# A two-layer hybrid decoder trunk: S5 preparation split into three steps, with its input projections and two gates spread over the attention heads

## The chip, the cores and the metric

The kernel runs on one core of one Trainium2 chip. The metric is the device time of one execution in microseconds (us). Shown for the kernel before are three timed runs and one profiled execution with its trace. The engines are TensorE (PE for its matmuls, PEld for its weight loads), VectorE (DVE), ScalarE (ACT), GpSimd (POOL) and SyncE (SP), which issues every DMA of this kernel.

## The reference, cut to what matters

Each of two layers normalises its input, makes one wide input projection of it, runs three token mixers side by side, gates and adds their outputs, projects the sum and adds it to the input. 512 tokens, width 1024, all in float32.

```python
for l in range(DEPTH):
    h = rms_norm(x, pre_norm[l])
    proj = h @ w_in[l]
    z_a, xbc, dt_raw, u_b, z_b, c_q, c_kv, k_rope, z_c, gate_logits = split_columns(proj)
    y_a = ssd_branch(z_a, xbc, dt_raw, ...) @ w_a[l]
    y_b = s5_branch(u_b, z_b, ...) @ w_b[l]
    y_c = mla_branch(c_q, c_kv, k_rope, z_c, ...) @ w_c[l]
    gates = jax.nn.sigmoid(gate_logits).reshape(bsz, s, N_BRANCH, D_MODEL)
    merged = gates[..., 0, :] * y_a + gates[..., 1, :] * y_b + gates[..., 2, :] * y_c
    x = x + rms_norm(merged @ w_o[l], post_norm[l])
```

The change touches two branches. MLA is latent attention with 16 heads: q and k/v come from normalised latents of rank 512 and 256, and each head runs a causal softmax over 512 positions. S5 is a complex diagonal state-space model over 64 groups of 16 channels with 64 states each. Its input is `u_b`, 1024 columns of the projection. The kernel computes it in chunks of 8 tokens: from powers of the diagonal it builds, for every group, a local response (kpad), an output operator (odr) and the state that each chunk adds (msd); a scan over 64 chunks follows later.

## The kernel before, in words

Every float32 operand is split into a high and a low part (`split`, line 83: an ACT copy and a DVE subtraction) and each product is three matmuls. `weight` (line 92) loads a 128x1024 weight tile into one of two `wf` buffers by a DMA on SP, and ACT and DVE (or, for every third tile in the MLA stage, POOL) split it; `dense` (line 108) then runs 24 matmuls of 512 columns into one of three main PSUM banks. `proj` (line 134) is `dense` on a tile of the input projection.

A layer (`layer`, line 980) runs two MLA latent projections and the small tail projection, then the MLA stage, then `mix` (line 1001): the softmax sums are divided out, the gates and output projections of MLA are merged, then SSD, S5 and the final projections. The S5 preparation, `s5_prep` (line 241), is a Python generator whose steps are placed among the attention work: `fill(n)` in `mla` (line 481) advances it n steps. It is called once before the latents (line 510), once between the two normalisations (line 513), and at the end of each head two times on even heads and three times on odd ones (line 601).

The first step computes the powers of the diagonal on DVE. Then each of eight blocks of eight groups takes five steps. `block(b)` (line 317) projects the S5 input tile, copies it to `pu`, writes it to DRAM (`ud`, line 322), reads it back in another order in eight DMAs of 16 partitions into `puf` (line 325), writes that to DRAM for later (`u2`, line 329), loads the B and C parameters `bc1`, `bc2` (lines 332 to 334), and forms `pbb`, `pbs` on POOL. `front(b, s)` (line 350), four times, builds on POOL the operators of two groups: `pw1`, `pv1`. `back(b, s)` (line 368), one step later, transposes `pw1` on PE into the bank `pm` (line 377), splits it into `pmh`, `pml`, multiplies these with the split input `pu2` into `pM` (lines 386, 387), and on every second step copies `pM` to `pmo`, makes the local responses `pk` (line 395, the same bank as `pm`), copies them to `pkf` and writes them to `kpad` (line 404). After four steps `pmo` goes to DRAM (line 406). `pu`, `puf` and `pmo` share two buffers (tag `pf`); `pmh` and `pml` have one each.

`gate` (line 446) projects one tile of gate logits and puts its tanh on ACT into one of seven shared `tmp` buffers; `gates_ahead` (line 452) makes gates that do not yet exist. `mix` begins with two MLA gates (line 1009).

The order written in Python is not the order on the engines. The kernel is built with `schedule_with_timeline_sim=True`: a planner orders the instructions of each engine by a simulated timeline, with the order written as priority, and each engine then works through its list in that fixed order. SP's DMA issues are such a list too.

## Time and profile before

| | us |
|---|---|
| median of 3 runs | 1980.36 (1975.66 to 1982.38) |
| the profiled execution | 1977.92 |
| its span, first to last instruction | 1976.1 |
| PE busy | 1870.3 (95%) |
| DVE busy | 1420.3 (72%) |
| ACT busy | 914.2 (46%) |
| POOL busy | 631.9 (32%) |
| mean granted TensorE clock | 0.967 |

The profiled execution is 2.4 us under the median, and 1.8 us of it lie outside the span. Busy time is counted per engine; matmuls overlap their weight loads, so PE and PEld stand side by side. A row of the windows view gives, for a stretch of the span, its length, the busy time of each engine with the number of instructions, the granted clock of PE as a share of full speed, the busy share of the DMA engines and the GB/s they moved. A row of the timeline gives start, length, engine, line, operation, tiles, shapes, count and, in brackets, the idle time before it and what ended it. A row of the waits view gives the total wait in us, how many waits, and the longest.

### The profile page before, as it was taken

To read this page: it belongs to the slowest core of one execution; us is meant where nothing else is said; L and a number is where in the kernel's file an instruction comes from. 1 tells how busy PE (TensorE), PEld (TensorE's weight loads), DVE (VectorE), ACT (ScalarE), POOL (GpSimd) and SP (SyncE) were. 2 spreads that over 40 slices of the span, in tenths; PEclk is the share of its full clock that TensorE was granted. 3 is DMA by queue.
4 is the path that set the end of the run, shared out by engine and by line. 5 is a ranking of instruction groups with operands and counts; after the bars stand their busy time and mean duration, and the time that the engine had idled before them with its cause. 6 is when DMAs were issued, how large, how long until landed. Compare 5 with 4: busy or idle time off the path is not lost.

```text
span 1976.1 us, 28153 instructions
## 1 busy us (share of the span) xinstructions
PE 1870.3 (95%) x9880; PEld 1528.1 (77%) x9880; DVE 1420.3 (72%) x2882; ACT 914.2 (46%) x1647; POOL 631.9 (32%) x679
## 2 busy tenths in 40 slices
PE   7898999899999989999998989999999999999998
PEld 5687777687877868888876877776878887788887
DVE  6866566799999857744578566667999996776443
ACT  4355455522555545533332555554235663554331
POOL 1746656201233201201118465661013331012010
PEclk9898998899999999999997999998999999999999
DMA  5343333322321266345233334343332224662541
GB/s 158 94 114 94 108 114 103 119 92 84 128 65 64 75 187 182 92 152 167 90 83 90 111 93 122 100 128 96 96 130 75 74 76 113 183 174 86 171 128 43
DMA packets 136253, 219.99 MB, mean 111 GB/s; under 512 B 39856, under 2 KB 79408, under 8 KB 135600
## 3 DMA queue, kind: packets, MB, share of 16 engines
q1 hardware_dynamic: 136112, 218.19, 37.1%
q8 instruction: 78, 1.28, 0.3%
q14 instruction: 63, 0.52, 0.1%
HBM read 182.08 MB, written 31.33 MB: 108 GB/s over the span
## 4 chain that ended last, share of the span: by engine, by line
PE 60%; DVE 22%; DMA 9%; ACT 3%; issue 2%; POOL 2%; SPq 2%; DVEq 0%; ACTq 0%; POOLq 0%
PE mm L116 15%; PE mm L117 14%; PE mm L119 14%; DMA wf<-in_w_in 3%; DVE wl L78 3%; DVE keep L69 3%; PE mm L61 2%; PE mm L62 2%; PE mm L63 2%; PE aux L61 1%; DVE tmp L69 1%; DVE ms L899 1%; PE aux L62 1%; PE aux L63 1%; DVE sc_t L896 1%
## 5 line engine op out<-in xcount | busy, mean ns | idle before, releaser
L116 PE MATMUL mm<-hh,wh 128*128 128x512 f32 (+1 forms) x1232 | 499.5, 405 | 11.5 <-ACT wh L66 8.0
L66 ACT ACTIVATE wh<-wf 128x1024 fp32r<-128x1024 f32 (+1 forms) x294 | 291.3, 994 | 440.2 <-PE mm L117 227.2
L117 PE MATMUL mm<-hl,wh 128*128 128x512 f32 (+1 forms) x1232 | 492.0, 399 | 0.0
L78 DVE TENSOR_TENSOR wl<-wf,wh 128x1024 fp32r<-128x1024 f32 (+1 forms) x243 | 294.8, 1218 | 188.1 <-ACT wh L66 154.3
L119 PE MATMUL mm<-hh,wl 128*128 128x512 f32 (+1 forms) x1232 | 314.9, 393 | 1.9 <-DVE wl L78 1.9
L116 PEld LDWEIGHTS mm<-hh,wh 128*128 128x128 f32 (+1 forms) x1232 | 236.5, 192 | 72.2 <-ACT wh L66 11.6
L117 PEld LDWEIGHTS mm<-hl,wh 128*128 128x128 f32 (+1 forms) x1232 | 236.2, 192 | 48.5 <-issue 0.5
L119 PEld LDWEIGHTS mm<-hh,wl 128*128 128x128 f32 (+1 forms) x1232 | 228.2, 188 | 52.6 <-DVE wl L78 2.3
L81 POOL TENSOR_TENSOR mg<-mg,tmp 128x512 f32<-128x512 f32 x32 | 77.7, 2431 | 458.1 <-DVE tmp L78 240.5
L81 POOL TENSOR_TENSOR wl<-wf,wh 128x1024 fp32r<-128x1024 f32 (+1 forms) x51 | 108.9, 2135 | 302.6 <-PE mm L119 209.3
L116 PE MATMUL mm<-ah,wh 128*128 128x512 f32 x512 | 200.3, 393 | 0.0
L117 PE MATMUL mm<-al,wh 128*128 128x512 f32 x512 | 199.9, 391 | 0.0
L119 PE MATMUL mm<-ah,wl 128*128 128x512 f32 x512 | 127.6, 390 | 0.0
L116 PEld LDWEIGHTS mm<-ah,wh 128*128 128x128 f32 x512 | 96.2, 188 | 21.4 <-ACT pkf L66 0.7
L117 PEld LDWEIGHTS mm<-al,wh 128*128 128x128 f32 x512 | 96.1, 188 | 20.9 <-issue 1.0
L119 PEld LDWEIGHTS mm<-ah,wl 128*128 128x128 f32 x512 | 95.7, 188 | 19.6
L617 DVE CUSTOM_DVE_ANT_0 sc<-aux,cmask 128x128 f32<-128x128 f32 (+3 forms) x128 | 60.9, 485 | 63.5 <-PE aux L63 62.5
L66 ACT ACTIVATE sc<-sc,nm 128x128 f32<-128x128 f32 (+3 forms) x128 | 70.4, 554 | 13.3 <-DVE nm L73 13.2
L81 POOL TENSOR_TENSOR pv<-pq,ar 128x288 f32<-128x288 f32 x64 | 49.1, 789 | 77.2 <-PE pk L395 68.7
L69 DVE SCALAR_TENSOR_TENSOR keep<-mm,cw,keep 128x511 f32<-128x511 f32 (+2 forms) x96 | 71.1, 740 | 2.0 <-ACT keep L66 1.5
L66 ACT ACTIVATE tmp<-mm 128x512 f32<-128x512 f32 x76 | 44.8, 592 | 56.2 <-PE mm L63 31.5
L81 POOL TENSOR_TENSOR pw<-pbb,ar 128x256 f32<-128x256 f32 x64 | 51.0, 799 | 41.8 <-PE pm L377 41.6
(346 smaller groups left out, 4002.8 us busy)
## 6 DMA issues: line engine op xcount, KB each, us to landing
wf<-in_w_in SPq DMA_DIRECT2D x156, 512.0 KB, 3.6
odr<-pv SPq DMA_DIRECT2D x64, 128.0 KB, 2.0
wf<-in_w_c SPq DMA_DIRECT2D x16, 512.0 KB, 3.4
wf<-in_w_a SPq DMA_DIRECT2D x16, 512.0 KB
wf<-kpad SPq DMA_DIRECT2D x128, 64.0 KB, 6.4
wf<-odr SPq DMA_DIRECT2D x16, 512.0 KB, 7.1
wf<-in_w_glu SPq DMA_DIRECT2D x16, 512.0 KB, 3.4
wf<-in_w_b SPq DMA_DIRECT2D x16, 512.0 KB, 3.8
```

Of the source, the lines that this page charges most:

```text
L61: mm(out, ah, bh, start=start, stop=False)
L62: mm(out, ah, bl, start=False, stop=False)
L63: mm(out, al, bh, start=False, stop=stop)
L66: self.nc.scalar.activation(out, in_, func, **kw)
L69: self.nc.vector.scalar_tensor_tensor(out, in0, s, in1, op0, op1)
L78: self.nc.vector.tensor_tensor(out, a, b, op)
L81: self.nc.gpsimd.tensor_tensor(out, a, b, op)
L116: mm(ps[:m], wh[:, o(i)], bh, start=i == 0, stop=False)
L117: mm(ps[:m], wh[:, o(i)], bl, start=False, stop=False)
L119: mm(ps[:m], wl[:, o(i)], bh, start=False, stop=i == k - 1)
L617: nc.vector.tensor_tensor_reduce(out=sc, in0=ps[:, :n], in1=self.cmask[:, 512 - n:512], op0=ALU.add, op1=ALU.max, scale=1.0, scalar=-3.0e3 ...
L896: nc.vector.tensor_tensor(t1, sc1, s, ALU.mult)
```

## The change

The S5 input projections leave the blocks. A new method `s5_u(l, pp, b)` projects tile b, copies it to `pu` and writes it to the DRAM tensor `u2` at once in the later order, in eight DMAs of 16 partitions and 256-byte pieces; `ud` and the way back through SBUF go. `inputs(n)` in `layer` makes the next n of them: two after the MLA latents are projected, one on every odd head until all eight are made. A block now begins with `load(b)`, which reads `u2` and the parameters two steps ahead of the block's first use. The five steps of a block become four. `back` becomes `operands` (transpose, split, local responses, `kpad`) and, one step later again, `states` (the products into `pM`, `pmo`, `msd`). `pu` and `pmo` no longer share buffers with `puf`; `puf`, `pmo`, `bc2`, `pmh` and `pml` have two buffers. `fill` is called two times at the end of every head. Two MLA gates are made in heads 14 and 15 with buffers `gk` of their own, not at the start of `mix`. The size of a scratch area for DMA descriptors in SBUF is set to 1024.

```diff
@@ -236,6 +236,16 @@
         pr = self.bank()
         nc.tensor.matmul(pr, self.ones, dg, start=True, stop=True)
         return pr
+
+    def s5_u(self, l, pp, b):
+
+        ps = self.proj(l, UB + b)
+        u = pp.tile([P, 512], F32, name="pu", tag="pu").rearrange("p (j c) -> p j c", j=8)
+        self.act_(u[:, ::-1], ps.rearrange("p (c j) -> p j c", j=8))
+        for g in range(8):
+            self.nc.sync.dma_start(
+                self.u2[b, :, 64 * g:64 * g + 64].rearrange("(j h) c -> h j c", j=8), u[16 * g:16 * g + 16],
+            )
 
 
     def s5_prep(self, l, pp):
@@ -301,40 +311,35 @@
...
         d = lambda nm, shape: self.dr.tile(shape, F32, name=f"{nm}{l}")
-        kpad, odr, msd, u2 = d("kpad", [16, 64, 240]), d("odr", [P, 64, P]), d("msd", [2, 64, 2, 32, 64]), d("u2", [8, P, 512])
-        ud = d("ud", [8, 8, 16, 8, 64])
+        kpad, odr, msd, u2 = d("kpad", [16, 64, 240]), d("odr", [P, 64, P]), d("msd", [2, 64, 2, 32, 64]), self.u2
...
         NB = 2
         et = self.gt
-        pf = lambda nm: pp.tile([P, 512], F32, name=nm, tag="pf", bufs=2)
 
         bbp = [pt(f"pbb{i}", [P, 8, 32]) for i in range(2)]
         for t in bbp:
             nc.gpsimd.memset(t, 0.0)
 
-        def block(b):
-
-            ps = self.proj(l, UB + b)
-            u = pf("pu").rearrange("p (j c) -> p j c", j=8)
-            self.act_(u[:, ::-1], ps.rearrange("p (c j) -> p j c", j=8))
-            nc.sync.dma_start(ud[b].rearrange("g h j c -> (g h) j c"), u)
-            uf = pf("puf")
-            for j in range(8):
-                nc.sync.dma_start(
-                    uf[16 * j:16 * j + 16].rearrange("h (g c) -> h g c", g=8),
-                    ud[b, :, :, j].rearrange("g h c -> h g c"),
-                )
-            nc.sync.dma_start(u2[b], uf)
+        def load(b):
+
+            uf = pt("puf", [P, 512], 2)
+            nc.sync.dma_start(uf, u2[b])
             g8 = slice(8 * b, 8 * b + 8)
-            x1, x2 = (pt(n, [P, 8, 2, 16]) for n in ("bc1", "bc2"))
+            x1, x2 = pt("bc1", [P, 8, 2, 16]), pt("bc2", [P, 8, 2, 16], 2)
             nc.sync.dma_start(x1, a["s5_bc"][l, :, g8])
             nc.sync.dma_start(x2[0:64], a["s5_bc"][l, 64:128, g8])
             nc.sync.dma_start(x2[64:128], a["s5_bc"][l, 0:64, g8])
+            return uf, x1, x2
+
+        def block(b, uf, x1, x2):
+
+            g8 = slice(8 * b, 8 * b + 8)
...
-            u1, bs, q1 = (pt(n, [P, 8, 16]) for n in ("pu1", "pbs", "pq1"))
+            u1 = pp.tile([P, 8, 16], F32, name="pu1", tag="pv2")
+            bs, q1 = (pt(n, [P, 8, 16]) for n in ("pbs", "pq1"))
...
@@ -365,18 +370,38 @@
             nc.sync.dma_start(odr[:, gs], v1[:, :, 1:9].rearrange("p g k h -> p g (k h)"))
             return keep["v"], w1
 
-        def back(b, s, uf, bb, v1, w1):
+        def operands(b, s, uf, bb, v1, w1):
+
             if s == 0:
-                u = keep["u"] = pp.tile([P, 8, 2, 64], F32R, name="pu2", tag="pu2")
+                u = keep["u"] = pp.tile([P, 8, 2, 64], F32R, name="pu2", tag="pu2", bufs=1)
                 self.split(uf.rearrange("p (g c) -> p g c", g=8), u[:, :, 0], u[:, :, 1])
-                keep["mo"] = pf("pmo").rearrange("p (g c) -> p g c", g=8)
-                nc.gpsimd.memset(keep["mo"][:, :, 0], 0.0)
-            u, mo = keep["u"], keep["mo"]
             pm = self.pq.tile([P, 512], F32, name="pm", tag="pb")
             for i in range(NB):
                 nc.tensor.transpose(pm[:, i * P:i * P + P], w1[:, i].rearrange("p k h -> p (k h)"), self.ident)
-            mh, ml = (pp.tile([P, NB * P], F32R, name=x, tag=x) for x in ("pmh", "pml"))
+            mh, ml = (pp.tile([P, NB * P], F32R, name=x, tag=x, bufs=2) for x in ("pmh", "pml"))
             self.split(pm[:, :NB * P], mh, ml)
+            if s % 2:
+                q = 4 * (s // 2)
+                pk = self.pq.tile([P, P], F32, name="pk", tag="pb")
+                for i in range(4):
+                    nc.tensor.matmul(
+                        pk[32 * i:32 * i + 32], bbp[b % 2][:, q + i], v1[:, i, 0:8].rearrange("p k h -> p (k h)"),
+                        start=True, stop=True, tile_position=(0, 32 * i),
+                    )
+                kf = pt("pkf", [P, P], 2)
+                self.act_(kf, pk)
+                n = 2 * b + s // 2
+                self.stt(kf[:, 0:16], self.diag, dT[:, n:n + 1], kf[:, 0:16], ALU.mult, ALU.add)
+                for i in range(4):
+                    nc.sync.dma_start(kpad[:, 8 * b + q + i, 112:240], kf[32 * i:32 * i + 16])
+            return b, s, keep["u"], mh, ml
+
+        def states(b, s, u, mh, ml):
+
+            if s == 0:
+                keep["mo"] = pt("pmo", [P, 512], 2).rearrange("p (g c) -> p g c", g=8)
+                nc.gpsimd.memset(keep["mo"][:, :, 0], 0.0)
+            mo = keep["mo"]
             if s % 2 == 0:
                 keep["pM"] = self.pq.tile([P, 4, 2, 64], F32, name="pM", tag="pM")
             pM = keep["pM"]
@@ -389,33 +414,23 @@
                 q = 4 * (s // 2)
                 self.act_(mo[:, q:q + 4, 1:64], pM[:, :, 0, 0:63])
                 self.tt(mo[:, q:q + 4, 1:64], mo[:, q:q + 4, 1:64], pM[:, :, 1, 0:63], ALU.add)
-
-                pk = self.pq.tile([P, P], F32, name="pk", tag="pb")
-                for i in range(4):
-                    nc.tensor.matmul(
-                        pk[32 * i:32 * i + 32], bbp[b % 2][:, q + i], v1[:, i, 0:8].rearrange("p k h -> p (k h)"),
-                        start=True, stop=True, tile_position=(0, 32 * i),
-                    )
-                kf = pt("pkf", [P, P], 2)
-                self.act_(kf, pk)
-                n = 2 * b + s // 2
-                self.stt(kf[:, 0:16], self.diag, dT[:, n:n + 1], kf[:, 0:16], ALU.mult, ALU.add)
-                for i in range(4):
-                    nc.sync.dma_start(kpad[:, 8 * b + q + i, 112:240], kf[32 * i:32 * i + 16])
             if s == 3:
                 nc.sync.dma_start(msd[b // 4, :, :, 8 * (b % 4):8 * (b % 4) + 8].rearrange("p r g c -> r p g c"), mo)
 
-        todo = None
+        todo, done, nxt = None, None, load(0)
         for b in range(8):
-            blk = block(b)
-            yield
+            blk = block(b, *nxt)
             for s in range(4):
                 vw = front(b, s, *blk)
-                if todo:
-                    back(*todo)
+                if done:
+                    states(*done)
+                done = operands(*todo) if todo else None
                 todo = (b, s, blk[0], blk[1], *vw)
+                if s == 2 and b < 7:
+                    nxt = load(b + 1)
                 yield
-        back(*todo)
+        states(*done)
+        states(*operands(*todo))
 
 
     def norm_in(self, tt, xt, G):
@@ -445,7 +460,7 @@
 
     def gate(self, l, i, m):
         ps = self.proj(l, GT + 8 * i + m)
-        t = self.tmp()
+        t = self.tp.tile([P, 512], F32, name="gk", tag="gk", bufs=2) if i == 2 and m < 2 else self.tmp()
         self.act_(t, ps, AF.Tanh, scale=0.5)
         return t
 
@@ -478,7 +493,7 @@
         self.gt(mg, mg, g, ALU.add)
 
 
-    def mla(self, l, fill):
+    def mla(self, l, fill, inputs):
         nc, tc, a = self.nc, self.tc, self.a
         with tc.tile_pool(name=f"mla{l}", bufs=1, reuse_waits="tile") as mp:
             qn, kvn = mp.tile([P, 4], F32, name="qn"), mp.tile([P, 2], F32, name="kvn")
@@ -509,6 +524,7 @@
 
             fill(1)
             cq, ckv = latent(CQ, 4), latent(CKV, 2)
+            inputs(2)
             cq = normed(*cq, qn, "cq")
             fill(1)
             ckv = normed(*ckv, kvn, "ck")
@@ -595,10 +611,13 @@
                     make_k(h // 2 + 1)
                 if h % 4 == 0:
                     make_v(h // 4)
+                if h % 2 == 1:
+                    inputs(1)
                 if h < 15:
                     pr[h + 1] = self.attend_qk(mp, q[h + 1], kt[(h + 1) % 2], h + 1)
                 values(h)
-                fill(3 if h % 2 else 2)
+                self.gates_ahead(l, 2, max(0, h - 13))
+                fill(2)
             self.lo_pool = 0
 
     def attend_qk(self, mp, q, k, h):
@@ -985,15 +1004,24 @@
         self.krdt = self.sm.tile([64, 512], F32, name="krdt")
         self.act_(self.krdt[0:48], ps[0:48])
         self.yc = []
+        self.gates, self.gdone = {}, [0, 0, 0]
         with ExitStack() as pst:
             pp = pst.enter_context(tc.tile_pool(name=f"prep{l}", bufs=1, reuse_waits="tile", side="right"))
+            self.u2 = self.dr.tile([8, P, 512], F32, name=f"u2{l}")
+            todo_u = list(range(8))
+
+            def inputs(n):
+                for b in todo_u[:n]:
+                    self.s5_u(l, pp, b)
+                del todo_u[:n]
+
             prep = self.s5_prep(l, pp)
 
             def fill(n):
                 for _ in range(n):
                     next(prep, None)
 
-            self.mla(l, fill)
+            self.mla(l, fill, inputs)
             fill(99)
         with tc.tile_pool(name=f"act{l}", bufs=8, reuse_waits="tile") as self.act:
             self.mix(l)
@@ -1005,7 +1033,6 @@
             mgp = self.mgp = mgs.enter_context(tc.tile_pool(name=f"mg{l}", bufs=1, reuse_waits="tile"))
             self.mg = [mgp.tile([P, 512], F32, name=f"mg{m}") for m in range(8)]
             self.yacts = []
-            self.gates, self.gdone = {}, [0, 0, 0]
             self.gates_ahead(l, 2, 2)
 
             nc.vector.reciprocal(self.rs, self.rs)
@@ -1219,7 +1246,7 @@
-    nc = bacc.Bacc("TRN2", target_bir_lowering=False, num_devices=1)
+    nc = bacc.Bacc("TRN2", target_bir_lowering=False, num_devices=1, dynamic_dma_scratch_size=1024)
```

## Rows read from the trace of the kernel before

**Rows 1.** The page, parts 1 and 2: engine totals; granted clock in 40 slices.

```profile
PE 1870.3 (95%) x9880; PEld 1528.1 (77%) x9880; DVE 1420.3 (72%) x2882; ACT 914.2 (46%) x1647; POOL 631.9 (32%) x679
...
PEclk9898998899999999999997999998999999999999
```

**Rows 2.** Windows: both MLA stages (first and third row) and all behind each.

```profile
62.00:388.00 326.00, 294.80 (x1576) 239.67 (x1574) 215.62 (x467) 169.13 (x391) 192.79 (x258) 0.92 0.35 103
388.00:1042.00 654.00, 637.61 (x3367) 521.83 (x3367) 493.35 (x959) 287.12 (x434) 118.48 (x76) 0.99 0.38 115
...
1042.00:1367.00 325.00, 295.02 (x1574) 239.50 (x1572) 221.39 (x487) 167.49 (x391) 200.40 (x263) 0.91 0.36 103
...
1367.00:1976.10 609.10, 594.64 (x3126) 487.16 (x3125) 444.29 (x815) 265.11 (x390) 108.89 (x65) 0.99 0.37 114
```

**Rows 3.** Windows: ten stretches of the MLA stages with idle PE and low clock.

```profile
75.20:90.00 14.80, 10.40 (x32) 7.59 (x33) 13.50 (x23) 4.59 (x9) 14.54 (x22) 0.65 0.46 136
178.00:192.00 14.00, 9.07 (x35) 7.35 (x36) 8.21 (x20) 6.97 (x18) 8.59 (x13) 0.63 0.34 107
238.00:250.00 12.00, 8.62 (x58) 7.77 (x57) 6.56 (x17) 4.34 (x11) 6.75 (x9) 0.86 0.48 125
322.00:337.00 15.00, 12.58 (x47) 9.99 (x46) 11.78 (x27) 9.34 (x22) 11.56 (x18) 0.66 0.38 119
360.00:388.00 28.00, 22.70 (x110) 15.84 (x109) 21.84 (x52) 15.39 (x37) 7.86 (x11) 0.82 0.19 53
1054.00:1072.00 18.00, 12.81 (x38) 8.88 (x37) 16.39 (x26) 4.79 (x10) 17.62 (x27) 0.62 0.39 110
1074.00:1087.00 13.00, 8.50 (x31) 6.11 (x30) 11.93 (x17) 3.71 (x8) 11.18 (x10) 0.74 0.25 71
1122.00:1132.00 10.00, 8.10 (x33) 5.85 (x31) 4.80 (x10) 7.18 (x17) 0.73 (x1) 0.83 0.51 152
...
1303.00:1316.00 13.00, 9.51 (x36) 7.43 (x36) 10.38 (x22) 8.13 (x19) 9.12 (x14) 0.74 0.41 113
1340.00:1367.00 27.00, 22.57 (x108) 16.64 (x106) 22.63 (x59) 14.68 (x36) 7.57 (x11) 0.75 0.20 54
```

**Rows 4.** Timeline of PE: three first matmuls behind a wait.

```profile
78.61 1.94 PE L237 MATMUL aux<-tmp,ones 128*128 128x512 f32 x2 [3.44 <-DVE tmp L73]
...
241.84 0.33 PE L61 MATMUL aux<-kh,qh 96*128 96x128 f32 x1 [3.38 <-DMA qh<-rrh]
...
1124.84 0.33 PE L386 MATMUL pM<-pu,pmh 128*128 128x128 f32 x1 [1.84 <-DVE pu L78]
```

**Rows 5.** Timeline of SP's DMA issues around 237 us.

```profile
234.43 0.41 SPq L322 DMA_DIRECT2D ud<-pu  x1
...
237.05 2.71 SPq L325 DMA_DIRECT2D puf<-ud  x6
239.86 1.20 SPq L550 DMA_DIRECT2D qh<-rrh  x2
```

**Rows 6.** Waits of PE over the whole span: the S5 operands.

```profile
PE pM L386 <- ACT pmh L66: 10.6, 11, 2.6
PE pm L377 <- ACT pkf L66: 9.9, 4, 3.7
...
PE pM L387 <- DVE pml L78: 5.3, 4, 4.2
```

**Rows 7.** Timelines of PE and ACT: the first layer's two MLA gates.

```profile
355.30 1.98 PE L119 MATMUL mm<-hh,wl 128*128 128x512 f32 x8
...
368.67 1.08 ACT L66 ACTIVATE tmp<-mm 128x512 f32<-128x512 f32 x2
```

**Rows 8.** A late weight tile: page part 6, then SP's and ACT's timelines.

```profile
wf<-in_w_in SPq DMA_DIRECT2D x156, 512.0 KB, 3.6
...
173.51 1.10 SPq L102 DMA_DIRECT2D wf<-in_w_in  x1
...
182.13 1.06 ACT L66 ACTIVATE wh<-wf 128x1024 fp32r<-128x1024 f32 x1 [4.68 <-DMA wf<-in_w_in]
```

## The prediction, made before the changed kernel ran

> **What bounds the kernel now.** I read the page first, then windows, then the waits and timelines inside the stretches that stood out. TensorE is busy 1870.3 us of the span, 95% [rows 1]. The change takes no matmul away, so it can only win what PE loses: idle time, and time at the lower of its two clock levels (a granted clock of 0.5 is 1.2 GHz, 1.0 is 2.4 GHz). The windows show where that is [rows 2]. In the first MLA stage, 62 to 388 us, PE idles 326 - 294.80 = 31.2 us at a granted clock of 0.92, so another 0.08 x 326 = 26 us of full-speed time are lost. In the second, 1042 to 1367 us, it is 30.0 us of idle time and 0.09 x 325 = 29 us. Together 61 us idle and 55 us of clock, 116 us. Behind each stage the clock is 0.99 and PE idles only 16.4 us of 654 and 14.5 us of 609. No other engine is full in the MLA stages: DVE is busy 66 and 68%, ACT 52%, POOL 59 and 62%. So PE waits there for chains across engines, and what the change is worth is read in these two stages alone.
>
> Ten stretches hold 84 us of the 116 [rows 3]. I price a stretch as its idle time plus (1 - clock) x length. The clock falls after an idle gap: after the 3.38 us gap that ends at 241.84 and after the 1.84 us one that ends at 1124.84 [rows 4] the stretches around them show 0.86 and 0.83 [rows 3]. A gap thus costs nearly twice its length: 116 / 61 = 1.9 on average.
>
> **The change part by part.**
>
> *Two S5 projections ahead of the latents' normalisation.* At 75.2 us PE has nothing until the row scale of the query latent is ready: 3.44 us [rows 4]. That stretch costs 4.4 + 0.35 x 14.8 = 9.6 us, its counterpart from 1054 us 5.2 + 0.38 x 18 = 12.0 us [rows 3], 21.6 us in all. One projection is 24 matmuls; eight take at most 1.98 us [rows 7], so one is 5.9 us. Before, one projection (block 0) can lie here; now there are two, and the extra one is longer than the gap. But DVE is busy 13.5 of 14.8 us and POOL 14.5 in the first of these stretches, so later gaps stay. I take half, 10.8 us, with bounds of 0 and 21.6.
>
> *The way through DRAM and back goes.* At 234.43 SP issues the write of `ud`, the read of it can only be issued at 237.05, six issues take 2.71 us, and the rope rows of q, for which PE stands still, come behind them at 239.86 [rows 5]. In the changed kernel nothing on SP waits for a landing between the two, and the read of `u2` comes a head later than its write. The stretches from 238 us (3.4 + 1.7 = 5.1 us) and from 1122 us (1.9 + 1.7 = 3.6 us, the split of `puf` late) [rows 3] have this cause. I take both, 8.7 us; bounds 0 and 8.7.
>
> *SP's own list.* A block had ten such issues: one store, eight reads, one store. It now has eight stores and one load. An issue over few partitions costs 2.71 / 6 = 0.45 us or 1.20 / 2 = 0.60 us, one over 128 partitions 0.41 [rows 5]. Before 2 x 0.41 + 8 x 0.45 = 4.4 us a block, now 0.41 + 8 x 0.45 to 0.60 = 4.0 to 5.2 us. Over 16 blocks that is 6 us less to 13 us more on a list that PE does not follow directly. I put it at nothing: weight tiles loaded one ahead hide it, and if that cover is gone it shows as the third rival below.
>
> *The states one step later, and two buffers for `pmh` and `pml`.* PE waits 10.6 us for `pmh` and 5.3 us for `pml` in front of the `pM` matmuls [rows 6]. With a whole step between split and use these waits end. Three stretches hang on them [rows 3]: from 322 us 2.4 + 5.1 = 7.5 us, from 1303 us 3.5 + 3.4 = 6.9 us, from 1074 us 4.5 + 3.4 = 7.9 us. In the third DVE is busy 11.93 of 13 us, so its list is behind whoever waits: I take half of it. Sum 7.5 + 6.9 + 3.9 = 18.3 us; bounds 0 and 22.3.
>
> *Two gates in the last heads.* Before, the planner already pulls both gates into the MLA stage: their last matmuls start at 355.30 in the first layer. But their tanh runs only at 368.67, two in a row [rows 7], which fits a wait for a shared `tmp` buffer; until then they hold two of three main PSUM banks, and PE has little to fill the end of the stage with. With buffers of their own the banks come free earlier, and a third gate can run there. The ends, from 360 and 1340 us, cost 5.3 + 5.0 = 10.3 us and 4.4 + 6.8 = 11.2 us [rows 3]. I take half, 10.7 us, as the softmax and the S5 tail keep their chain; bounds 0 and 21.5. That heads 12, 13 and 15 lose their projections costs nothing as far as the gates stand in for them, 5.9 us each.
>
> *What the change adds.* The local responses `pk` now follow the split of `pm` in the same step and the same bank, where before the state products lay between. So `pk` takes the wait over. Before, 15 waits of 15.9 us in all came with 64 splits [rows 6], 0.25 us a split; 32 `pk` groups give 8.0 us, with the clock (x 1.9) 15.2 us. Bounds: nothing, where the planner always puts other matmuls between, and 7.5 waits at the 7.5 us of the stretch from 322 us, 56 us. I take 15.2, as the nearest rows are the same split's. The wait of PE for `pkf`, 9.9 us [rows 6], stays, since `pm` and `pk` still share one bank; so does the stretch from 178 us (4.9 + 5.2 = 10.1 us [rows 3]), where ACT is held by a late weight tile. The more even buffers for `puf`, `pmo` and `bc2` and the scratch size carry no price of their own: they remove waits of POOL and SP, which are not full.
>
> **The sum.** 10.8 + 8.7 + 18.3 + 10.7 - 15.2 = 33.3 us less. The profiled execution has 1977.92 us and would come to 1944.6; it lies 2.4 us under the median of the runs, and on the median I forecast 1947.
>
> **The rivals.**
>
> *The idle time only moves.* ACT, DVE and SP keep their fixed lists, planned on a simulated timeline; a gap that is filled in one place opens at the next late weight tile. For it: ACT's wait of 4.68 us for a tile [rows 8] has nothing to do with S5's own chain, and the gates were already pulled forward. Then only the round trip's 8.7 us go, and something like half of that comes back: 1974 to 1984.
>
> *All of it goes.* The full bounds of the gains, 21.6 + 8.7 + 22.3 + 21.5 = 74 us, with the new `pk` wait at 8 us: about 66 us less, 1914. For it: all four causes stand next to each other in the rows, and 32 us of the 116 lie in smaller stretches that a looser chain also helps. Against: DVE and POOL are nearly full in the first stretches.
>
> *Slower: the stores of 256-byte pieces hold up the weights.* Place: SP's queue, behind the eight stores of `s5_u`. A weight tile lands 3.6 us after its issue at the median, but the one issued at 173.51 was split only at 182.13, 8.6 us later [rows 8]; on its way it had small transfers in front of it, and it cost PE 10.1 us [rows 3]. It decides as soon as a tile comes later than one projection's 5.9 us of PE work. If six of the 16 tiles' stores do that, 61 us come on top of the forecast: about 2008. For it: the weights use the same queue, and only two `wf` buffers lie ahead. Against: the eight reads before had pieces of the same size and the same count of issues. The Trainium skill, "DMA: Bandwidth & Descriptors", Specifications, says that a transfer below 512 B is not at line rate because the DMA engine reads, modifies and writes; it speaks against this change, since pieces of 256 B are now written, not read. By that rule this rival's 2008 stands in place of 1947; no row read here times such a store by itself.
>
> That the change does less than it says is part of the first rival: since a planner sets the order, projections and gates may land where they were.
>
> **How the numbers follow.** A measurement of this kernel can tell about 0.3%, 6 us, from no change. The forecast gets 0.55: five waits have a named cause that the edit takes away, and the price of the new one is from rows of the same tiles. Its own range is 1925 to 1970. All of it goes: 0.14. The idle time only moves: 0.13, of which 0.12 lie within 6 us of before. The slower rival gets 0.13, and the upper bound of the `pk` wait (56 us in place of 15.2: 1988) 0.05. Faster is 0.55 + 0.14 + 0.01 = 0.70, same 0.12, slower 0.18. The range runs from 1908 to 1990: below lies the part of the second case in which smaller stretches go as well, above most of the slower rival, together under 0.2.
>
> **What would show it.** Right: the MLA stages shorter by some 15 us each at a granted clock of 0.95 or more, with all behind them as long as before; no wait of PE for `pmh`, `pml` or rope rows; PE busy from 62 us on until the key latent; gates' tanh right behind their matmuls. New and expected: some waits in front of `pk`. Wrong: PE waiting for `wh` in the stages, weight tiles landing after more than 6 us (the slower rival), or stages of the old length with the gaps elsewhere (the first).

## The result, and the profile after

The forecast was 1947 us, faster. The changed kernel took **1990.6 us** at the median (1984.26 to 1993.63), the kernel before 1976.7 in the same set: a ratio of 1.0062, 95% interval [1.0044, 1.008]. It is slower, by 0.4 to 0.8%, and lies just above the range.

The profiled execution took 1992.71 us with a span of 1990.6. Its page, parts 1 and 2, in answer to [rows 1]:

```profile
PE 1867.5 (94%) x9880; PEld 1521.0 (76%) x9880; DVE 1415.4 (71%) x2882; ACT 916.6 (46%) x1647; POOL 628.9 (32%) x679
...
PEclk9989989899999999999998999998999999999999
```

Its windows in answer to [rows 2], with the same four stretches (the stages end some 20 us behind the heads, as there):

```profile
62.00:393.70 331.70, 292.03 (x1566) 235.40 (x1566) 210.70 (x470) 168.29 (x389) 196.61 (x257) 0.92 0.38 100
393.70:1052.00 658.30, 642.37 (x3379) 525.15 (x3378) 495.26 (x957) 290.01 (x435) 117.68 (x78) 0.99 0.37 111
1052.00:1378.30 326.30, 289.53 (x1561) 232.30 (x1560) 215.82 (x477) 168.00 (x390) 195.82 (x261) 0.93 0.39 102
1378.30:1990.60 612.30, 596.46 (x3137) 488.86 (x3136) 448.37 (x826) 265.49 (x391) 108.07 (x65) 0.99 0.36 110
```

The MLA stages, which were to be some 15 us shorter each, are 5.7 and 1.3 us longer. PE idles 39.7 us in the first (31.2 before) and 36.8 in the second (30.0), and the granted clock is where it was. What lies behind the stages was to stay as it was and is 4.3 and 3.2 us longer. The waits of PE, in answer to [rows 6] (total, times, longest):

```profile
PE aux L1053 <- DVE keep L78: 14.5, 2, 7.6
PE aux L61 <- DMA qh<-rrh: 14.3, 6, 3.1
...
PE pM L411 <- ACT pmh L66: 10.1, 6, 5.1
PE aux L237 <- DVE tmp L73: 9.5, 2, 5.3
...
PE pM L412 <- DVE pml L78: 4.3, 9, 0.9
...
PE pk L387 <- DVE pml L78: 1.6, 5, 0.4
```

Three things stand out, and each got experiments.

**The normalisation of the latents.** In the first layer DVE scales the key latent from 106.5 us on (97.5 before), first in the changed kernel, then in the kernel before:

```profile
106.45 1.39 DVE L69 SCALAR_TENSOR_TENSOR keep<-keep,kvn,aux 128x512 f32<-128x512 f32 x2
```

```profile
97.46 1.39 DVE L69 SCALAR_TENSOR_TENSOR keep<-keep,kvn,aux 128x512 f32<-128x512 f32 x2
```

PE's timeline: the sums of squares (L231), then the products that spread the row scale (L237), first in the changed kernel:

```profile
74.29 0.95 PE L231 MATMUL aux<-ones,tmp 128*128 128x1 f32 x8
...
85.27 2.00 PE L237 MATMUL aux<-tmp,ones 128*128 128x512 f32 x2 [4.20 <-DVE tmp L73]
```

In the kernel before, the sums ran at 62.98:

```profile
62.98 0.95 PE L231 MATMUL aux<-ones,tmp 128*128 128x1 f32 x8
```

The projections of the first two blocks now stand ahead of the sums and push them back by 11.3 us. The scale then comes 11.0 us behind the sums (15.6 before), with one projection in between and 4.20 us of idle time left (3.44 [rows 4]). So the fill was moved from inside the wait to ahead of it. What is left of the wait lies mostly on POOL. DVE has the mean squares ready at 76.15, and POOL takes their root at 82.95, behind work on S5's operators:

```profile
76.00 0.15 DVE L75 TENSOR_SCALAR rs_v<-aux 128x4 f32<-128x4 f32 x1
82.95 1.03 POOL L81 TENSOR_TENSOR rs_r<-rs_v,mhalf 128x4 f32<-128x4 f32 x1
```

Those 6.8 us were 8.3 before in this layer; in the second they are 5.9, and 0.9 before.

**Rope rows.** Six waits for q's rope rows, 14.3 us, where one of 3.38 us stood [rows 4]. SP's list shows why: eight stores of `u` for 6.61 us, and the rope rows behind them. It is so at six places of the span, with 6.61 to 7.67 us of stores.

```profile
169.87 6.61 SPq L246 DMA_DIRECT2D u<-pu  x8
...
177.56 1.52 SPq L566 DMA_DIRECT2D qh<-rrh  x2
```

**The start of the mix.** PE waits 7.55 us at 389.09 and 6.97 in the second layer for the `yc` products on DVE. In DVE's list the scan's first step now stands ahead of them, and waits there for the 2 MB of states, which SP asks for at 379.48:

```profile
387.42 0.27 DVE L915 TENSOR_TENSOR sc_t<-sc,ms 128x64 f32<-128x64 f32 x1 [6.96 <-DMA ms<-msd]
```

Better than forecast: PE no longer waits for `pkf`, a wait of 9.9 us that was to stay. What went as forecast: in the heads the waits for `pmh` are nearly gone (two of 5.1 and 2.8 us in the normalisation make up most of the 10.1; for `pml` 4.3 us are left), and a gate's tanh runs right behind its matmuls, in answer to [rows 7]:

```profile
353.90 0.60 ACT L66 ACTIVATE gk<-mm 128x512 f32<-128x512 f32 x1 [0.61 <-PE mm L119]
```

### The profile page after: what moved, and what is told of

It reads as the page before. It is cut to its first block, busy times and chain, and to the rows that moved or that the text cites. A ratio compares the mean times of both kernels' runs of the same rounds, so it can differ in the third digit from the quotient of the medians.

```text
span 1990.6 us, 28045 instructions
## 1 busy us (share of the span) xinstructions
PE 1867.5 (94%) x9880; PEld 1521.0 (76%) x9880; DVE 1415.4 (71%) x2882; ACT 916.6 (46%) x1647; POOL 628.9 (32%) x679
## 4 chain that ended last, share of the span: by engine, by line
PE 56%; DVE 24%; DMA 11%; POOL 3%; issue 3%; ACT 2%; SPq 1%; DVEq 0%; POOLq 0%; ACTq 0%
PE mm L116 13%; PE mm L117 13%; PE mm L119 12%; DVE wl L78 4%; DMA wf<-in_w_in 3%; PE mm L61 2%; PE mm L62 2%; DVE keep L69 2%; PE mm L63 2%; DMA msd<-pmo 2%; DVE ms L918 2%; DVE sc_t L915 2%; PE aux L61 1%; PE aux L62 1%; PE aux L63 1%
## 5 line engine op out<-in xcount | busy, mean ns | idle before, releaser
L78 DVE TENSOR_TENSOR pl<-aux,ph 128x512 fp32r<-128x512 f32 (+1 forms) x96 | 54.7, 592 | 9.4 <-ACT ph L66 8.8
```

The costliest lines, as they stand in the source:

```text
L78: self.nc.vector.tensor_tensor(out, a, b, op)
```

## The experiments

Times are medians; "against before" is the ratio to the kernel before in the same set, whose own median lay between 1974.3 and 1976.7, and its interval. The ratios are of means. The changed kernel was timed in the first of five sets alone. Between kernels of different sets, differences of the medians carry what the kernel before moved as well, up to 2.4 us, so the text gives the difference by the ratios beside them where the two disagree (0.1% is 2 us).

| kernel | us | against before |
|---|---|---|
| changed kernel | 1990.6 | 1.0062 [1.0044, 1.008] |
| scan_held | 1988.8 | 1.0072 [1.0051, 1.0094] |
| load_held | 1986.7 | 1.0062 [1.0048, 1.0077] |
| gatesmix_held | 1998.1 | 1.012 [1.01, 1.0139] |
| wide_store | 1975.2 | 1.0001 [0.9989, 1.0013] |
| act_stores | 1978.0 | 1.0019 [1.0005, 1.0033] |
| pu_two | 1987.1 | 1.0071 [1.0049, 1.0092] |
| norm_one | 1985.6 | 1.0062 [1.0043, 1.0081] |
| norm_first | 1968.2 | 0.9962 [0.995, 0.9975] |
| norm_load | 1979.1 | 1.0025 [1.0015, 1.0036] |
| norm_load_nolag | 1991.0 | 1.0077 [1.006, 1.0095] |
| norm_load_even | 1989.7 | 1.0077 [1.0062, 1.0091] |
| norm_late | 1974.1 | 0.9991 [0.9979, 1.0003] |
| norm_reads | 1982.2 | 1.0039 [1.0025, 1.0053] |
| norm_wide | 1960.1 | 0.993 [0.9916, 0.9945] |
| norm_act | 1960.3 | 0.9933 [0.9918, 0.9947] |
| norm_act_pu | 1983.8 | 1.0055 [1.0036, 1.0075] |

Where the time lies, from the profiled executions, in us and both layers added. The start ends with ACT's copy of the first layer's last latent projection. The normalisations run from that copy to DVE's first scaling of the key latent, the heads from there to the reciprocal of the softmax sums. The rest, up to the second layer's last latent projection and to the span's end, is called behind the heads.

| kernel | start | normalisations | heads | behind the heads |
|---|---|---|---|---|
| before | 63.7 | 69.3 | 538.7 | 1304.4 |
| changed kernel | 64.1 | 83.3 | 531.5 | 1311.7 |
| norm_first | 63.0 | 62.0 | 534.1 | 1307.7 |
| norm_one | 64.7 | 75.0 | 534.0 | 1310.6 |
| act_stores | 63.2 | 79.8 | 522.1 | 1308.3 |
| norm_act | 63.8 | 58.4 | 526.2 | 1310.8 |
| load_held | 63.7 | 83.9 | 521.7 | 1313.1 |

The kernel before makes one S5 projection in each normalisation, all others of the table two, so that their heads have one fewer (5.4 us of PE). An edit also moves stretches that it does not touch, since the planner orders all anew: load_held's edit lies behind the heads, and its heads are 9.9 us shorter than the changed kernel's. A few us in the heads are no proof of a cause by themselves.

### The normalisation

**norm_first**: the projections behind the norm. (The expectations call them the third block's; the call is that of the first two blocks.)

```diff
-            inputs(2)
             cq = normed(*cq, qn, "cq")
+            inputs(2)
```

> The changed kernel, with the third S5 block's projections called behind the normalisation of q instead of ahead of it, as in the kernel before. Theory A (the projections ahead take nothing away but push the sums of squares back, and S5's operator work stands ahead of the reciprocal root on POOL): the normalisation's gaps of 4.20 and 5.28 us shrink, the first norm's end comes back from 106.5 to about 98 to 101, and the time falls by 6 to 14 us, to about 1977 to 1985. Theory B (POOL's and VectorE's operator instructions set the norm whatever stands ahead on TensorE): the end of the norm stays at 104 to 107 and the time within 4 us of 1990.6.

1968.2 us, 22 us less by the medians and 20 by the ratios, more than theory A asked for, and faster than the kernel before. PE's timeline, then POOL's root and DVE's scaling of the key latent:

```profile
62.35 0.95 PE L231 MATMUL aux<-ones,tmp 128*128 128x1 f32 x8
...
76.53 1.84 PE L237 MATMUL aux<-tmp,ones 128*128 128x512 f32 x2 [3.55 <-DVE tmp L73]
...
72.67 1.02 POOL L81 TENSOR_TENSOR rs_r<-rs_v,mhalf 128x4 f32<-128x4 f32 x1
...
93.24 1.39 DVE L69 SCALAR_TENSOR_TENSOR keep<-keep,kvn,aux 128x512 f32<-128x512 f32 x2
```

The sums are back at 62.35, and two projections lie in the wait again. DVE scales the key latent from 93.2 on (106.5 in the changed kernel). The two normalisations take 62.0 us and not 83.3: 21.3 of the 23.8 us by which the span is shorter. So nearly all of the gain lies there. It does not hang on one plan: with both calls ahead, seven kernels take 39.0 to 44.0 us for each normalisation, and with both behind, nine take 28.2 to 32.6. POOL's root also comes sooner behind the mean squares (3.0 us, 6.8 in the changed kernel); moving it ahead in POOL's list by itself was not tried.

**pu_two** and **norm_one** ask why: in the changed kernel ACT stands 8.12 us at the second projection's eviction, until the stores have read the one buffer `pu`.

```diff
-        u = pp.tile([P, 512], F32, name="pu", tag="pu").rearrange("p (j c) -> p j c", j=8)
+        u = pp.tile([P, 512], F32, name="pu", tag="pu", bufs=2).rearrange("p (j c) -> p j c", j=8)
```

> The changed kernel, with two buffers for the tile pu of the projections ahead and not one. Theory A (the two projections stand ahead of q's sums of squares on TensorE, so that nothing is left to fill the wait behind them): the sums still begin at about 74, the norm's end stays at 104 to 107, and the time is within 5 us of 1990.6. Theory B (ACT stands 8.1 us at the second projection's eviction, until the eight stores have read the one buffer, with the norm's work behind it): that wait goes, the end of the norm comes back to about 98 to 101 and the time falls by 8 to 18 us.

```diff
-            inputs(2)
+            inputs(1)
             cq = normed(*cq, qn, "cq")
+            inputs(1)
```

> The changed kernel, with one of the first two blocks' projections called ahead of q's normalisation and one behind it. With both ahead the time is 1990.6, with both behind it 1968.2. Theory A (what stands ahead of the sums pushes them back, projection by projection): the sums begin about 5.5 us earlier than with both ahead, and the time lies between, 1975 to 1984. Theory B (the second projection's wait for the one pu buffer is the cause): with the second one behind the norm all of it is gone, 1965 to 1972.

With two buffers ACT evicts the second tile at 75.70, so its wait is gone, but the sums stay at 75.51 and the norm ends at 105.7:

```profile
75.51 0.95 PE L231 MATMUL aux<-ones,tmp 128*128 128x1 f32 x8
85.47 1.12 PE L237 MATMUL aux<-tmp,ones 128*128 128x512 f32 x2 [3.19 <-DVE tmp L73]
...
75.70 0.60 ACT L66 ACTIVATE pu<-mm 128x512 f32<-128x512 f32 x1 [1.18 <-PE mm L119]
```

1987.1: theory B falls. With one projection ahead the sums begin at 69.41, 4.9 us earlier, as A has it, but the time is 1985.6: by the medians 5 us of the 22, by the ratios nothing (1.0062 as in the changed kernel). That is above A's window and far above B's. The normalisations take 75.0 us, so 8.3 of the 21.3 us come back there; the heads are 2.4 us longer. ACT still stands 7.17 us at the second projection's eviction here, so norm_one by itself says nothing on B. Why so little of that reaches the time is not settled.

### SP's list

**wide_store**, and **norm_wide** with the same edit on top of norm_first:

```diff
-        for g in range(8):
-            self.nc.sync.dma_start(
-                self.u2[b, :, 64 * g:64 * g + 64].rearrange("(j h) c -> h j c", j=8), u[16 * g:16 * g + 16],
-            )
+        self.nc.sync.dma_start(self.u2[b], u.rearrange("p j c -> p (j c)"))
```

> The changed kernel, with the eight stores of u2 of 256-byte pieces put together to one store of 1 KB rows; u2 then lies in another order, so S5's input data is permuted and the output is not the reference's. Theory A (the eight small stores hold up the rope rows of the next pair on SP's queue): the six waits of aux on qh from rrh, 14.3 us in all, fall under 4 us, TensorE's clock beside them rises, and the time falls by 10 to 18 us, to about 1973 to 1981. Theory B (the rope rows are late because the projections of the same head push the make-ready of k itself back, on TensorE, ACT and VectorE): the six waits keep over 9 us and the time stays within 4 us of 1990.6.

> The kernel with the third block's projections behind q's normalisation, with the eight stores of u2 put together to one of 1 KB rows (u2 in another order, so S5's data is permuted and the output is not the reference's). In that kernel the waits of TensorE on the rope rows are gone, but six waits of aux on mx, 22.4 us in all, stand there, behind a weight that comes 4.2 to 4.4 us late to ACT and VectorE. Theory A (the stores' time on SP and in the DMA queues is what makes rope rows or weights late, whichever comes next): those six waits fall under 8 us and the time falls by 10 to 18 us from 1968, to 1950 to 1958. Theory B (the weights are late by their own buffers, freed late by the projections ahead): the waits stay over 15 us and the time within 4 us of 1968.

1975.2, 15 us less (12 by the ratios): theory A. The work is the same, but S5's input lies in another order, so the outputs of these two kernels are not the reference's. The six waits fall from 14.3 to 6.0 us. On norm_first the edit saves 8 us (6 by the ratios; 1960.1), short of A's window, and the waits on `mx` stay at 21.4 us where A had under 8. In norm_first these come from a weight tile that is late on ACT (4.39 us at 247.34), not from rope rows; the stores are only part of that. Nor were the waits on rope rows gone in norm_first, as the expectation says: they were 5.5 us, so the place of the norm alone takes most of the 14.3.

**act_stores**, and **norm_act** with the same edit on norm_first, keep the data in order:

```diff
-            self.nc.sync.dma_start(
+            self.nc.scalar.dma_start(
                 self.u2[b, :, 64 * g:64 * g + 64].rearrange("(j h) c -> h j c", j=8), u[16 * g:16 * g + 16],
             )
```

> The changed kernel, with the eight stores of each block's u issued by ACT and not by SP, all else as it is. Theory A (the stores' place in SP's list, ahead of rope rows and weights, is a cause by itself): the six waits on rope rows, 14.3 us in all, fall under 6 us and the time falls by 8 to 15 us, to 1975 to 1983. Theory B (the two causes are one, and with the norm late as it is the stores cost nothing): within 4 us of 1990.6. Theory C (in the norm ACT's issues, 7 to 8 us for eight, stand in the way of the norm's splits): above 1995.

> The kernel with the third block's projections behind q's normalisation, with the eight stores of u2 issued by ACT, which has just written them, and not by SP. Theory A (it is SP's list in which the stores stand in the way): SP's weights and rope rows come out ahead of them, the six waits on mx fall under 8 us, and the time falls by 5 to 15 us, to 1953 to 1963. Theory B (ACT's issues stand ahead of splits and exponentials and cost as much there, 8 times 6 blocks of 0.05 to 0.5 us a layer): 1968 to 1985.

1978.0 and 1960.3: 12.6 and 7.9 us less (8 and 6 by the ratios), theory A in both. PE's waits on rope rows in norm_first, wide_store and act_stores:

```profile
PE aux L61 <- DMA qh<-rrh: 5.5, 5, 2.3
PE aux L61 <- DMA qh<-rrh: 6.0, 6, 2.1
PE aux L61 <- DMA qh<-rrh: 0.8, 1, 0.8
```

They fall from 14.3 to 0.8 us in act_stores, whose pieces are as small as before. So it is the place in SP's list that makes the rope rows late. norm_act is **the best kernel of the study that computes the whole of it: 0.9933 of before [0.9918, 0.9947]**, 25 to 30 us below the changed kernel. Each gain alone is of the size that a new plan can make; that all four kernels with other stores gain speaks for the cause. By which wait the stores cost time on norm_first is less sure: norm_wide takes the same time with 21.4 us of waits on `mx`, where norm_act has 4.3. It is not free on ACT, as its timeline in norm_act shows:

```profile
70.33 8.04 ACTq L246 DMA_DIRECT2D u<-pu  x8
79.67 1.29 ACT L66 ACTIVATE cqh<-keep 128x512 fp32r<-128x512 f32 x2 [9.38 <-DMA u<-pu]
```

ACT stands there for eight issues. It can afford it: in norm_first it waited 6.00 us at the same place, for DVE's scaled latent.

**norm_act_pu** adds the second `pu` buffer:

> The first two blocks' projections behind q's normalisation, the stores issued by ACT, and two buffers for pu. Theory A (with the projections behind the norm, the wait for the one buffer lies beside other work): within 4 us of 1960. Theory B (it still holds ACT up there, and in the heads): 4 to 10 us below 1960.

1983.8, neither. The norm ends nearly as early (94.9 against 92.1), but the heads take 279 us and not 268 in the first layer and 278 and not 258 in the second, with PE's waits for `wh` at 19.8 us (10.3). What a 2 KB buffer per partition changes in the planned order or the memory layout there stays open.

**norm_reads** brings the old way through DRAM back, a step ahead:

```diff
-        for g in range(8):
-            self.nc.sync.dma_start(
-                self.u2[b, :, 64 * g:64 * g + 64].rearrange("(j h) c -> h j c", j=8), u[16 * g:16 * g + 16],
-            )
+        self.nc.sync.dma_start(self.ud[b].rearrange("g h j c -> (g h) j c"), u)
...
-            nc.sync.dma_start(uf, u2[b])
+            for j in range(8):
+                nc.sync.dma_start(
+                    uf[16 * j:16 * j + 16].rearrange("h (g c) -> h g c", g=8),
+                    self.ud[b, :, :, j].rearrange("g h c -> h g c"),
+                )
+            nc.sync.dma_start(u2[b], uf)
```

> The kernel with the third block's projections behind q's normalisation, with the way through DRAM of the kernel before: u goes out in one store, comes back in eight loads of 256-byte pieces (now a step ahead, in the staggered preparation), and goes to u2 in one store. Theory A (256-byte pieces cost more when they are written, 6.3 to 7.4 us for eight in the heads, than when they are read, 2.7 to 3.7 us): the time falls by 4 to 12 us from 1968, to 1956 to 1964. Theory B (the eight issues count, written or read, and one store more adds to them): within 4 us or up to 8 us above 1968.

1982.2, 14 us more: above B's window. Pieces of 256 bytes show no dearer when written: eight issues in a row take 3.63 to 7.96 us as reads here and 3.66 to 7.74 as stores in norm_first, and a store lands after 1.8 us at the median there, a read after 2.0 in the kernel before. But SP's own waits show two, the reads for the store and the store to `u2` for the reads, where norm_first has one of 8.1 us, the load of `u2` for the stores (total, times, longest):

```profile
SPq L330 <- DMA puf<-ud: 15.6, 8, 6.4
SPq L326 <- DMA ud<-pu: 13.1, 11, 1.7
```

While SP stands there, nothing behind it on its list is issued. PE's waits on `mx` grow from 22.4 us in norm_first to 35.6. That SP's waits make up all of the 14 us was not tried by itself.

**norm_load_even** (on norm_load, below) and **norm_late** (on norm_first) move the calls in the heads:

```diff
-                if h % 2 == 1:
+                if h % 2 == 0:
                     inputs(1)
```

> As the second kernel of this call, with the projections ahead called in even heads and not in odd ones, where the rope rows of the next pair of heads are made. Theory A (the eight stores stand ahead of the rope rows on SP in odd heads): the waits of aux on qh or on its bank's reader in the heads, 5 to 28 us there, fall under 4 us, and the time falls by 4 to 10 us. Theory B (with the normalisation put back the stores no longer come at the rope rows' time): within 4 us. Theory C (even heads have the values' products to make, so that the projection pushes those back): 3 to 10 us slower.

```diff
-                if h % 2 == 1:
-                    inputs(1)
...
                 values(h)
+                if h % 2 == 1:
+                    inputs(1)
```

> The kernel with the third block's projections behind q's normalisation, with the projections of the odd heads called behind the head's values and not ahead of the next head's scores. Theory A (the stores and the projection's weight are issued at the rope rows' time because of where the call stands): the waits on rope rows, mx and weights in the heads, 28 us, fall under 15 us and the time falls by 4 to 12 us. Theory B (the planner places them by its own due times): within 4 us of 1968.

Even heads cost 10.6 us (theory C): POOL's chains come late, with waits of PE on POOL's `wl` (9.6 us) and `pw` (9.2 us) that norm_load does not have. Behind the values (norm_late) it is 5.9 us more; neither theory had that.

### Gates and the start of the mix

**scan_held** and **gatesmix_held** (the same edit, and the gates out of the heads; the last line of the cut is gatesmix_held's alone, and its two gates use `tmp` again):

```diff
+        for t in (t1, t2):
+            nc.vector.tensor_copy(t.rearrange("p r g -> p (r g)"), self.yc[-1][:, 0:64])
         for c in range(63):
...
-                self.gates_ahead(l, 2, max(0, h - 13))
```

> The changed kernel, with two tiny copies on VectorE that tie the scan's temporaries to the last normalised MLA tile, so that the scan's first step stands behind the yc products. Theory A (the planner, with S5's operators done early, puts the scan ahead of the yc products in VectorE's list, and the scan waits there for the 2 MB of states): the gap of 7.55 us on TensorE behind the heads (389.09) and the one of 6.97 us in the second layer go, the wait of aux on keep falls from 14.5 us in all to under 3, and the time falls by 10 to 18 us, to about 1973 to 1981. Theory B (the gap is the missing gates' place: with two gates gone from the mix's start nothing fills it): the gap only changes its releaser, to the reciprocal r or to the gate's products, and the time stays within 4 us of 1990.6.

> The changed kernel, with the scan held behind the yc products as in the other kernel, and all MLA gates back at the mix's start (none in the last heads). Theory A (the gates in the last heads are near neutral, as they give TensorE the same matmuls in another place): within 4 us of the kernel with the scan held. Theory B (the gates fill the gap behind the heads, so that moving them out cost it): 5 to 12 us faster than the kernel with the scan held. Theory C (the gates fill waits of the last heads as intended): 5 to 11 us slower than it.

scan_held came to 1988.8, by number as theory B, but A's edit had not reached its aim: the gap is still 6.60 us, now because DVE waits until 386.11 for `a_log` (7.05 us), which SP issues behind the same load of states. The gates' part is the difference between the two: without them in the heads 9.4 us more, theory C.

**load_held** (and **norm_load**, on norm_first) ties the load itself:

```diff
+        nc.vector.tensor_copy(ms[:, 0, 0, 0:8], self.yc[-1][:, 0:8])
         nc.sync.dma_start(ms, msd.rearrange("h p r g c -> (h p) r g c"))
```

> The changed kernel, with one tiny copy on VectorE from the last normalised MLA tile into the first column of the scan's tile, ahead of the 2 MB load of the states, so that SP issues this load behind the small loads of the SSD tables and not ahead of them. Theory A (the load of the states, which waits on SP for the last stores of the states, holds up the small tables a_log, conv_w and conv_b behind it, and VectorE's fixed list waits for those or for the states ahead of the yc products): a_log lands before 380 in the first layer, both gaps of aux on keep, 14.5 us in the changed kernel and 13.7 with the scan alone held back, fall under 4 us in sum, and the time falls by 8 to 16 us, to about 1975 to 1982. Theory B (the gap is the room that the two gates left at the mix's start): the gap goes to another releaser and the time stays within 4 us of 1989 to 1990.

> The changed kernel with the third block's projections behind q's normalisation and the load of the states held back. Theory A (the two causes lie in stretches of their own and add): what the load saves in the changed kernel comes off here too, less the one gap that this order of the heads had already lost, 4 to 14 us below the kernel with the normalisation alone put back, so 1954 to 1965. Theory B (that kernel had no idle time left at the mix that mattered): within 4 us of 1968.

The gaps on `keep` are gone, and little or less than nothing is won: 1986.7 (by the ratios nothing) where A had 1975 to 1982, and 11 us **more** on norm_first. Windows of the second layer, 0 to 40, 160 to 220 and 220 to 280 us behind the heads' end, the changed kernel first, then load_held:

```profile
1358.90:1398.90 40.00, 29.59 (x116) 21.44 (x117) 30.61 (x103) 13.33 (x20) 0.00 (x0) 0.83 0.28 88
...
1518.90:1578.90 60.00, 60.00 (x361) 49.97 (x360) 59.04 (x100) 33.81 (x57) 19.64 (x13) 1.00 0.23 71
1578.90:1638.90 60.00, 60.00 (x328) 49.11 (x328) 58.93 (x94) 34.82 (x57) 24.93 (x17) 1.00 0.24 71
```

```profile
1344.30:1384.30 40.00, 35.79 (x140) 26.07 (x141) 32.56 (x101) 14.95 (x22) 0.00 (x0) 0.91 0.29 100
...
1504.30:1564.30 60.00, 57.14 (x322) 46.08 (x321) 56.54 (x91) 32.26 (x53) 18.24 (x13) 1.00 0.23 70
1564.30:1624.30 60.00, 57.72 (x321) 46.94 (x320) 53.33 (x84) 31.64 (x51) 19.15 (x14) 0.97 0.22 71
```

PE wins 6.2 us of work in the first 40 us and loses 5.1 in the two later windows, where DVE had been busy 59 of 60 us and now is 57 and 53. From the heads' end to that layer's first `ys` it is 348.6 us (337.4 in the changed kernel); in the first layer 339.5 (346.8), so there the gain of 7.3 stays. What one layer wins the other gives back. Whether the later scan does this by itself, or the new order that the planner makes behind it, wasn't separated.

### The staggering

**norm_load_nolag**, on norm_load:

```diff
-                if done:
-                    states(*done)
-                done = operands(*todo) if todo else None
+                if todo:
+                    states(*operands(*todo))
```

> As the kernel before it in this call, with the states' products called in the same step as their operands, as in the kernel before, and not one step later. Theory A (the staggering hides the wait for the split of the transposed operators on ACT and VectorE, 10.6 and 5.3 us before): the waits of pM on pmh and pml come to 10 us or more, and the time is 6 to 18 us above the kernel beside it. Theory B (the planner, by its costs and due times, places the products late enough itself, so that the step's place in the text says little): within 4 us of it.

11.8 us more, A's size, but not by A's waits: `pM` on `pmh` and `pml` comes to 1.0 us (0.9 in norm_load). The heads are longer (95.1 to 371.9 us against 94.3 to 363.1) at a granted clock of 0.91 against 0.93. That the kernel with the staggering is some 10 to 12 us faster is shown; that this comes by ending those waits is not.

## Why the prediction was wrong

**The step that failed is the first, "Two S5 projections ahead of the latents' normalisation"** (-10.8 us, at worst 0). I took it that a projection called ahead fills the gap of [rows 4]. It stood ahead of the sums that start the wait, and delayed them by 11.3 us in the first layer. The two normalisations came out 14.0 us longer than before. Of that one more projection in each, which the heads no longer hold, is 10.9 us (5.44 us each on PE's timeline), so even with it counted out nothing was won. With the calls behind the norm, as in norm_first, the fill works: the same stretches are 7.3 us shorter than before, extra projection included. The bound of 0 was wrong in kind: I had let work that is added ahead of a chain's start cost nothing. The prediction saw POOL busy 14.5 of 14.8 us there and halved the gain for it, but did not ask behind what the root stands in POOL's list.

By the spans the change was to save 33.3 us and cost 14.5, a miss of 48. The place of the calls is 20 to 22 us of it (norm_first). Even norm_act, which puts the stores right as well, is only 13 us faster than before.

**"SP's own list" was put at nothing**, with loads of weights one ahead as cover. The cover was the wrong one: rope rows are waited for directly. Off SP the stores are worth 8 to 13 us in the changed kernel and 6 to 8 on norm_first. The third rival had the place (behind the stores in SP's list), but its victim was the rope rows and not the weights (PE's largest wait for `wh` is 8.7 us in all, 8.0 before), and at its price (61 us, so 2008) it lay too high. Its other ground was the row of the Trainium skill, "DMA: Bandwidth & Descriptors", Specifications, that a transfer under 512 B is not at line rate. No run here shows the written pieces slower than the read ones: issues alike, landing after 1.8 and 2.0 us.

**The way through DRAM** (-8.7) was right in sign. Compared on norm_first with the old way, also a step ahead, the new one is 14 us better, above the bound. **The states a step later** (-18.3): 10 to 12 us for the step alone, in its bounds, though by another way than those waits. **Two gates** (-10.7): 9.4 us, right. **The new wait for `pk`** (+15.2) is 1.6 us in all, near the lower bound; at the prediction's own factor of 1.9 that is 3 us. This term was some 12 us too dear, and by luck it brought the forecast nearer to the result.

These parts do not add up to what was measured. The heads are 7.2 us shorter, less than the 10.9 us of the projections that left them, though the three gains just named, each measured alone on its own kernel, come to some 35. What lies behind the heads was to stay as it was and is 7.2 us longer. What took that up is open. Of the rivals, "the idle time only moves" had the direction but not the sign. What I did not price at all is the start of the mix, a gap of 7 us in each layer; closing it in load_held left the ratio at 1.0062, and the time behind the heads as long, so it is not where the time went.

## What to carry to other kernels

Work called ahead to fill a wait must stand behind the instruction that starts the wait, not ahead of it: look on the bounding engine for what begins the chain, and on the other engines for what each link of it waits behind. Count a DMA that is moved not by its bytes but by who stands behind it on its queue's list; another engine's queue may be free for that time. A gap that an edit opens is a cost only when closing it shortens the run: here two gaps of 7 us were closed and next to nothing was won.

## What was not expected of the hardware

Eight small stores issued by ACT keep it for 5.32 to 10.87 us around the normalisations (norm_act and act_stores; 70.33 above: 8.04), where SP takes 3.83 to 4.42 for the same four groups in the changed kernel, and the kernel is still faster.
